# Two quads of weights multiplied in plain fp32, and the loads of w_ada spread among them

## The chip, the cores and the metric

One core of one Trainium2 chip runs the kernel. The metric is the device time of one execution in microseconds (us); less is better. A core has TensorE (PE, with its weight loads as PEld), VectorE (DVE), ScalarE (ACT), GpSimd (POOL) and SyncE (SP), which here issues the transfers.

## What the reference computes

One decoder layer on 256 tokens of width 2048, in fp32:

```python
mod = jax.nn.silu(c) @ w_ada + b_ada                # w_ada 2048 x 6144
shift, scale, gate = jnp.split(mod, 3, axis=-1)
h = _rms_norm(x, g_norm) * (1.0 + scale[:, None, :]) + shift[:, None, :]
proj = h @ w_in                                     # w_in 2048 x 9296
...                                                 # 8 + 8 heads: DSA top-k and MoBA attention, SiLU gates
y = jnp.concatenate([ya, yb], axis=-1) @ w_out      # w_out 2048 x 2048
return x + gate[:, None, :] * y
```

`h` can't be multiplied before the columns of `w_ada` that make its shift and scale have been loaded and summed.

## The kernel before

**Units.** The 2048 inputs of `w_in` are 16 k-tiles of 128 rows. Its columns are 19 groups: z, q, k, v of four quads (b0, b1, a0, a1), 512 columns each, and three index groups i0, i1, i2 of 384, 384 and 336. The unit of the schedule is one k-tile by 512 columns; the projection has 290.5 of them.

**Split products.** An fp32 number is kept as two parts in fp32r: `hi`, a copy rounded by ACT, and `lo`, the rest, made by DVE. A product of weights and `h` is the three matmuls hi*hi, hi*lo, lo*hi (L760, L761, L762) for each of the two tiles of 128 tokens (t). Weights are split by `cast_hi` (L306, ACT, into `wh`) and `cast_lo` (L316, DVE, into `wl`), two cast units ahead of the matmuls (`LA`); `h` is split in `build_h` (L391, L392, L397 for k-tile 0; L394, L395, L397 after).

**Modulation.** A load of w_ada holds 128 of its columns over all rows (1 MB); `gemv` (L273, DVE) sums it with s = silu(c). Chunk 0 is k-tile 0, chunk 1 k-tile 1, then two k-tiles each, with a shift and a scale load for each k-tile. Once a chunk's last sum is there, its k-tiles of h are built.

**Passes.** A planner, run while the program is built, orders the loads. A column group takes, in its turn, those k-tiles whose modulation is known, and adds the result to what it had (`evac`: the first pass copies on ACT, L662; later ones add on DVE, L664). A quad whose four groups take one k-tile is one load of 1 MB, "a quad"; both first quads, b1 and a0, are of this kind with k-tile 0. When all 16 k-tiles are known, the turns go by `FINAL`, and attention runs between the matmuls of this last stretch. The output projection follows.

**Buffers and queues.** All loads of w_ada, w_in and w_out share four buffers of 1 MB (`raw`); SP issues them in their order, each when the load four before it has been used up: by `gemv`, or by the last `cast_lo`. `wh` and `wl` have four buffers each, the products' PSUM tiles (`mm`) four. In the start, `in_order` fixes the order of instructions on the engines: x is scaled by its rsqrt (L350), transposed on PE (L360, `ptx`) and copied with the gain (L365, `xnT`).

Of the kernel before, what the change touches and what calls it, by code (L numbers as in the profile page):

```python
# [49 lines left out]
def hybrid_block(ctx: ExitStack, tc: tile.TileContext, x, cols, w_ada_t, w_in, w_out, out):  # L50
# [58 lines left out]
    # s = silu(c), and the products of the head gains with -1/sqrt(HD)  # L109
# [23 lines left out]
    def rsqrt(dst, ssq, n):  # L133
        # dst = (ssq / n + eps) ** -0.5
# [9 lines left out]
    # a load of w_ada: 128 of its columns, over all rows; h0, h1 bound the part of the rows  # L144
# [38 lines left out]
    while turn:  # L183
        while ready and (ready[0][0] <= n_kt or known == pos[turn[0]]):
# [38 lines left out]
    # the first weights come before the last part of the first chunk of the modulation  # L223
# [5 lines left out]
    def issue(upto):  # L229
        nonlocal n_issued  # L230
        while n_issued < min(upto, len(loads)):
            ld = loads[n_issued]
            raw = rawp.tile([P, 2048], F32, tag="raw", name=f"raw{n_issued}")
# [6 lines left out]
            elif ld["kind"] == "quad":  # L240
                # the column groups of a quad are 1024 apart
# [5 lines left out]
                if n_issued == n_start - 1:  # L247
                    # its first group, and the others behind the next load
# [42 lines left out]
    def cast_hi(j):  # L291
# [62 lines left out]
    def x_transpose(k2):  # L354
        # the transpose of two k-tiles of x, each token scaled by its rsqrt
# [13 lines left out]
    def start_mod():  # L369
        # what is known of the first chunk's modulation before its last part  # L370
# [108 lines left out]
    def prep(q, c):  # L479
        # sums of squares of the heads, their rsqrt, and the scaled heads (in place)  # L480
# [160 lines left out]
    with in_order():  # L641
        for j in range(1, LA):
# [161 lines left out]
```

## Time and profile before

| what | us |
|---|---|
| median of 3 runs | 579.33 |
| their range | 578.39 to 579.95 |
| span of the profiled execution | 577.5 |
| PE busy | 550.7 |
| DVE busy | 443.4 |
| ACT busy | 325.4 |

No time of its own is given for the profiled execution: its span, 577.5, runs from its first to its last record, and the median of the runs, 579.33, stands 1.8 above it. Busy times overlap, so they don't add to the span.

### The profile page before, as it was taken

How to read it: one execution, taken by the hardware profiler on the slowest of the kernel's cores; microseconds unless marked ns; L12 is line 12 of the kernel's file. 1: busy time of each engine (PE TensorE's matmuls, PEld its weight loads, DVE VectorE, ACT ScalarE, POOL GpSimd, SP SyncE). 2: the span in 40 equal slices, each digit the busy share in tenths (PEclk: the TensorE clock that was granted, in tenths of full speed). 3: DMA queues.
4: the chain of work that ended last, by engine and by line, in shares of the span. 5: the costliest groups of instructions: out<-in, count | busy, mean ns of one | idle time of the engine just before them, and what ended most of it. 6: DMA issues, size and time to landing. Idle time of an engine off the chain costs nothing.

```text
span 577.5 us, 7394 instructions
## 1 busy us (share of the span) xinstructions
PE 550.7 (95%) x2626; PEld 457.4 (79%) x2626; DVE 443.4 (77%) x675; ACT 325.4 (56%) x667; POOL 49.3 (9%) x61
## 2 busy tenths in 40 slices
PE   2869999999999999998999999999999999999996
PEld 2548888888878998976768888888877888887885
DVE  4876879898899797888979995788668576458452
ACT  5898563434435353567655567555766785554340
POOL 4100000000000000102101012010330210000000
PEclk8789999999999999999999999999999999999999
DMA  8988988989998898887864476777556468445701
GB/s 290 370 298 316 396 330 305 337 322 345 351 346 273 338 344 315 306 312 268 297 236 159 150 276 239 247 281 273 212 182 219 146 228 282 145 150 190 245 36 36
DMA packets 59669, 150.08 MB, mean 260 GB/s; under 512 B 3056, under 2 KB 9456, under 8 KB 53616
## 3 DMA queue, kind: packets, MB, share of 16 engines
q1 hardware_dynamic: 58480, 147.51, 71.4%
q10 hardware_dynamic: 1152, 2.10, 1.2%
q8 instruction: 20, 0.33, 0.2%
q14 instruction: 17, 0.14, 0.1%
HBM read 147.50 MB, written 2.10 MB: 259 GB/s over the span
## 4 chain that ended last, share of the span: by engine, by line
PE 80%; ACT 8%; DVE 4%; DMA 3%; POOL 2%; issue 2%; SPq 0%; DVEq 0%; ACTq 0%; POOLq 0%
PE mm_y_o L760 5%; PE mm_y_o L761 5%; PE mm_y_o L762 5%; PE mm_h_qa L760 2%; PE mm_h_ka L761 2%; PE mm_h_qa L762 2%; PE mm_h_qa L761 2%; PE mm_h_ka L762 2%; PE mm_h_ka L760 2%; PE mm_h_za L761 2%; PE mm_h_i L760 2%; PE mm_h_zb L762 2%; PE mm_h_zb L761 2%; PE mm_h_qb L760 2%; PE mm_h_qb L761 2%; PE mm_h_qb L762 2%
## 5 line engine op out<-in xcount | busy, mean ns | idle before, releaser
L306 ACT ACTIVATE wh<-raw 128x1024 fp32r<-128x1024 f32 (+3 forms) x192 | 187.1, 993 | 158.2 <-DMA raw<-in_w_in 60.6
L316 DVE TENSOR_TENSOR wl<-raw,wh 128x1024 fp32r<-128x1024 f32 (+3 forms) x192 | 215.2, 1140 | 61.9 <-ACT wh L306 61.4
L273 DVE CUSTOM_DVE_ANT_0 raw<-raw,s_row 128x2048 f32<-128x2048 f32 (+1 forms) x49 | 110.6, 2257 | 13.9 <-DMA raw<-in_w_ada_t 13.8
L760 PE MATMUL mm_y_o<-wh,yT 128*128 128x512 f32 x128 | 51.7, 404 | 0.0
L761 PE MATMUL mm_y_o<-wl,yT 128*128 128x512 f32 x128 | 49.9, 390 | 0.0
L762 PE MATMUL mm_y_o<-wh,yT 128*128 128x512 f32 x128 | 49.8, 390 | 0.0
L760 PE MATMUL mm_h_i<-wh,hhi 128*128 128x384 f32 (+1 forms) x96 | 31.5, 333 | 0.5 <-DVE p_i L664 0.5
L762 PE MATMUL mm_h_i<-wh,hlo 128*128 128x384 f32 (+1 forms) x96 | 31.5, 329 | 0.0
L761 PE MATMUL mm_h_i<-wl,hhi 128*128 128x384 f32 (+1 forms) x96 | 31.5, 328 | 0.0
L760 PE MATMUL mm_h_za<-wh,hhi 128*128 128x512 f32 x64 | 26.3, 413 | 4.6 <-ACT wh L306 4.6
L762 PEld LDWEIGHTS mm_y_o<-wh,yT 128*128 128x128 f32 x128 | 24.0, 188 | 5.3 <-DVE yT L554 0.2
L760 PEld LDWEIGHTS mm_y_o<-wh,yT 128*128 128x128 f32 x128 | 24.1, 188 | 4.8 <-ACT yT L553 0.2
L761 PEld LDWEIGHTS mm_y_o<-wl,yT 128*128 128x128 f32 x128 | 24.1, 188 | 4.6
L760 PE MATMUL mm_h_kb<-wh,hhi 128*128 128x512 f32 x64 | 26.0, 406 | 0.2 <-ACT p_zb L662 0.2
L760 PE MATMUL mm_h_vb<-wh,hhi 128*128 128x512 f32 x64 | 25.7, 403 | 0.2 <-ACT p_qb L662 0.2
L760 PE MATMUL mm_h_zb<-wh,hhi 128*128 128x512 f32 x64 | 25.9, 408 | 0.0
L761 PE MATMUL mm_h_za<-wl,hhi 128*128 128x512 f32 x64 | 25.7, 402 | 0.1
L760 PE MATMUL mm_h_qb<-wh,hhi 128*128 128x512 f32 x64 | 25.7, 401 | 0.0
L760 PE MATMUL mm_h_qa<-wh,hhi 128*128 128x512 f32 x64 | 25.7, 409 | 0.0
L760 PE MATMUL mm_h_ka<-wh,hhi 128*128 128x512 f32 x64 | 25.4, 402 | 0.0
L762 PE MATMUL mm_h_za<-wh,hlo 128*128 128x512 f32 x64 | 25.3, 398 | 0.0
L760 PE MATMUL mm_h_va<-wh,hhi 128*128 128x512 f32 x64 | 25.2, 397 | 0.0
(215 smaller groups left out, 1208.4 us busy)
## 6 DMA issues: line engine op xcount, KB each, us to landing
raw<-in_w_in SPq DMA_DIRECT2D x51, 1024.0 KB, 6.0
raw<-in_w_ada_t SPq DMA_DIRECT2D x47, 1024.0 KB, 6.7
raw<-in_w_out SPq DMA_DIRECT2D x16, 1024.0 KB, 5.1
raw<-in_w_in SPq DMA_DIRECT2D x17, 512.0 KB, 4.5
raw<-in_w_in SPq DMA_DIRECT2D x11, 768.0 KB, 6.2
x<-in_x SPq DMA_DIRECT2D x8, 256.0 KB, 6.9
xr<-in_x ACTq DMA_DIRECT2D x8, 256.0 KB, 6.5
raw<-in_w_in SPq DMA_DIRECT2D x3, 672.0 KB, 5.5
```

What stands on the lines that cost most here:

```text
L273: nc.vector.tensor_tensor_reduce(out=ld["v"], in0=ld["v"], in1=s_row[:, h0:h1], scale=1.0, scalar=0.0, op0=ALU.mult, op1=ALU.add, accum_ou ...
L306: nc.scalar.activation(hi[:, :n, :w], v, AF.Copy)
L316: nc.vector.tensor_tensor(lo[:, :n, :w], v, sb["hi"][:, :n, :w].bitcast(F32), op=ALU.subtract)
L760: nc.tensor.matmul(ps, a_hi, sb["hi"][:, i, :w], start=st, stop=False)
L761: nc.tensor.matmul(ps, a_hi, sb["lo"][:, i, :w], start=False, stop=False)
L762: nc.tensor.matmul(ps, a_lo, sb["hi"][:, i, :w], start=False, stop=en)
```

## The change

Both first quads are loaded into buffers of the pool that holds the weights' parts (one tile now holds `hi` and `lo` together, four buffers as before), not into `raw`, and their products are single matmuls of plain fp32 (`whole`): no cast, and `h` of k-tile 0 not split until the fifth cast unit (`SPLIT_AT`), when `split_h(0)` makes the parts for the later passes. The loads of w_ada come at places of their own (`ADA_FIRST`), where four stood together; chunk 1 counts as known once its loads are placed, and loads of w_ada are pulled forward where the next group could otherwise take no new k-tile. Removed comments are left out here.

```diff
-ADA_AT, ADA_FIRST, ADA_GAP, ADA_LAG, GATE_AT, GATE_GAP = 4, 4, 5.5, 2, 150, 8
+ADA_FIRST, ADA_GAP, ADA_LAG, GATE_AT, GATE_GAP = (4, 8, 8, 11, 14.5, 18), 5.5, 2, 150, 8
...
+    def w_tile(name):
+        return wsp.tile([P, 2, 2, 512], F32R, tag="w", name=name)
...
+    ada_at = list(ADA_FIRST)
+    ada_at += [ADA_FIRST[-1] + ADA_GAP * (i + 1) for i in range(len(ada) - len(ada_at))]
...
-        if ada and n_kt >= ada_at:
-            for _ in range(ADA_FIRST if ada_at == ADA_AT else 1):
-                ld = ada.pop(0)
-                loads.append(ld)
-                if "end" in ld:
-                    ready.append((n_kt + ADA_LAG, CHUNKS[ld["end"]][1]))
-            ada_at += ADA_GAP
+        if ada and n_kt >= ada_at[0]:
+            ada_at.pop(0)
+            ld = ada.pop(0)
+            loads.append(ld)
+            if "end" in ld:
+                ready.append((n_kt + (ADA_LAG if ld["end"] > 1 else 0), CHUNKS[ld["end"]][1]))
...
     while turn:
+        while ada and (n_kt >= ada_at[0] or (known == pos[turn[0]] and not ready)):
+            ada_at[0] = min(n_kt, ada_at[0])
+            between()
...
-            raw = rawp.tile([P, 2048], F32, tag="raw", name=f"raw{n_issued}")
+            if ld["kind"] == "quad":
+                raw = w_tile(f"quad{n_issued}").rearrange("p c k n -> p (c k n)").bitcast(F32)
+            else:
+                raw = rawp.tile([P, 2048], F32, tag="raw", name=f"raw{n_issued}")
...
+        if sb["whole"]:
+            return
...
-        hi = wsp.tile([P, 2, 512], F32R, tag="wh", name=f"wh{j}")
-        nc.scalar.activation(hi[:, :n, :w], v, AF.Copy)
-        sb["hi"] = hi
+        sb["hi"], sb["lo"] = w_tile(f"w{j}").rearrange("p c k n -> c p k n")
+        nc.scalar.activation(sb["hi"][:, :n, :w], v, AF.Copy)
...
-            hhi[k] = h_tile(f"hhi{k}", F32R)
             if b == 0:
-                nc.scalar.activation(hhi[k], xnT[k], AF.Identity, bias=sh, scale=am)
                 nc.vector.tensor_scalar(xnT[k], xnT[k], am, sh, op0=ALU.mult, op1=ALU.add)
...
+    SPLIT_AT = 4
...
+        if j == SPLIT_AT:
+            with in_order():
+                split_h(0)
...
+            if sb["whole"]:
+                nc.tensor.matmul(ps, xnT[k][:, ts_], ld["v"][:, i, :w], start=st, stop=en)
+                continue
             nc.tensor.matmul(ps, a_hi, sb["hi"][:, i, :w], start=st, stop=False)
```

Line numbers move: L391/L392 become L409, L397 becomes L392, L306 L320, L316 L330, L662 L675, L664 L677, L273 L284, and the plain products stand in L782.

**The first quad on PE.** Names are tiles: `mm_h_zb` is the product of group z of quad b1, `ptx` the transposes of x. Before, from the fifth matmul of the first quad on:

```order
L761 MATMUL mm_h_zb_0_265<-wl_218,hhi_242 128x512
L760 MATMUL mm_h_zb_1_266<-wh_216,hhi_242 128x512
L762 MATMUL mm_h_zb_0_265<-wh_216,hlo_245 128x512
L761 MATMUL mm_h_zb_1_266<-wl_218,hhi_242 128x512
L762 MATMUL mm_h_zb_1_266<-wh_216,hlo_245 128x512
L760 MATMUL mm_h_qb_0_292<-wh_247,hhi_242 128x512
L761 MATMUL mm_h_qb_0_292<-wl_249,hhi_242 128x512
L762 MATMUL mm_h_qb_0_292<-wh_247,hlo_245 128x512
L360 MATMUL ptx_277<-ident,x_2_154 128x128 x2
L760 MATMUL mm_h_qb_1_293<-wh_247,hhi_242 128x512
L761 MATMUL mm_h_qb_1_293<-wl_249,hhi_242 128x512
L360 MATMUL ptx_277<-ident,x_2_162 128x128 x2
```

In the changed kernel, from just before the quad's first product:

```order
L373 MATMUL ptx_227<-ident,x_1_152 128x128 x2
L782 MATMUL mm_h_zb_0_249<-quad_173,xnT_216 128x512
L373 MATMUL ptx_227<-ident,x_1_160 128x128 x2
L373 MATMUL ptx_232<-ident,x_1_152 128x128 x2
L373 MATMUL ptx_232<-ident,x_1_160 128x128 x2
L782 MATMUL mm_h_zb_1_250<-quad_173,xnT_216 128x512
L373 MATMUL ptx_257<-ident,x_2_154 128x128 x2
L373 MATMUL ptx_257<-ident,x_2_162 128x128 x2
L782 MATMUL mm_h_qb_0_268<-quad_173,xnT_216 128x512
L782 MATMUL mm_h_qb_1_269<-quad_173,xnT_216 128x512
```

Three matmuls for a group and tile of tokens have become one, of `xnT` itself, and the first stands among the transposes that used to come ahead of it.

**From the second quad to the first two-k-tile pass, on ACT.** Before, behind the last gains (`raw_317` is the second quad, `raw_319` the first weights of the next pass):

```order
L365 ACTIVATE xnT_389<-ptx_380,cc 128x256
L306 ACTIVATE wh_331<-raw_317 128x512
L306 ACTIVATE wh_364<-raw_317 128x512
L306 ACTIVATE wh_391<-raw_317 128x512
L306 ACTIVATE wh_407<-raw_317 128x512
L662 ACTIVATE p_za_0_403<-mm_h_za_0_395 128x512
L662 ACTIVATE p_za_1_405<-mm_h_za_1_396 128x512
L306 ACTIVATE wh_425<-raw_319 128x1024
L662 ACTIVATE p_qa_0_419<-mm_h_qa_0_411 128x512
```

In the changed kernel (`raw_289` is that next pass's first load):

```order
L378 ACTIVATE xnT_329<-ptx_320,cc 128x256
L390 ACTIVATE hhi_331<-xnT_216 128x256
L675 ACTIVATE p_za_0_339<-mm_h_za_0_335 128x512
L675 ACTIVATE p_za_1_341<-mm_h_za_1_336 128x512
L411 ACTIVATE xnT_239<-xnT_239,mmod_291 128x256
L675 ACTIVATE p_qa_0_347<-mm_h_qa_0_343 128x512
L390 ACTIVATE hhi_373<-xnT_239 128x256
L675 ACTIVATE p_qa_1_349<-mm_h_qa_1_344 128x512
L320 ACTIVATE w_360<-raw_289 128x1024
L675 ACTIVATE p_ka_0_367<-mm_h_ka_0_363 128x512
L675 ACTIVATE p_ka_1_369<-mm_h_ka_1_364 128x512
```

The casts of the quads are gone; the split of h (`hhi_331`) now stands here, and the first cast, `w_360`, stands behind the copies of the second quad's z and q (four of its eight) and ahead of those of k.

**The loads behind the quads, on SP and DVE.** Before, SP's loads from the first two-k-tile one on (`in_w_ada_t` is w_ada):

```order
L260 DMA raw_319<-in_w_in 128x2x512
L237 DMA raw_321<-in_w_ada_t 128x2048
L260 DMA raw_323<-in_w_in 128x2x512
L260 DMA raw_423<-in_w_in 128x2x512
L260 DMA raw_441<-in_w_in 128x2x512
L237 DMA raw_443<-in_w_ada_t 128x2048
L260 DMA raw_462<-in_w_in 128x2x336
L260 DMA raw_486<-in_w_in 128x2x384
L260 DMA raw_510<-in_w_in 128x4x384
L237 DMA raw_512<-in_w_ada_t 128x2048
```

In the changed kernel, from the second two-k-tile one on; `raw_353` is the scale of k-tile 2, `raw_390` and `raw_439` shift and scale of k-tile 3:

```order
L271 DMA raw_351<-in_w_in 128x2x512
L248 DMA raw_353<-in_w_ada_t 128x2048
L271 DMA raw_355<-in_w_in 128x2x512
L271 DMA raw_377<-in_w_in 128x2x512
L248 DMA raw_390<-in_w_ada_t 128x2048
L271 DMA raw_392<-in_w_in 128x2x336
L271 DMA raw_416<-in_w_in 128x2x384
L248 DMA raw_439<-in_w_ada_t 128x2048
L271 DMA raw_441<-in_w_in 128x2x384
L271 DMA raw_465<-in_w_in 128x2x512
```

And DVE there, from the split of h of k-tile 1 on (an ISA row with a `raw` is a product of w_ada, the row behind it reads its sum):

```order
L392 TENSOR_TENSOR hlo_375<-xnT_239,hhi_373 128x256
L330 TENSOR_TENSOR w_360<-raw_289,w_360 128x1024
L330 TENSOR_TENSOR w_379<-raw_351,w_379 128x1024
L284 ISA raw_353,mmod_358<-raw_353,s_row 128x2048
L284 ISA mmod_358 128x1
L330 TENSOR_TENSOR w_395<-raw_355,w_395 128x1024
L330 TENSOR_TENSOR w_418<-raw_377,w_418 128x1024
L284 ISA raw_390,mmod_358<-raw_390,s_row 128x2048
L284 ISA mmod_358 128x1
L330 TENSOR_TENSOR w_444<-raw_392,w_444 128x2x336
L330 TENSOR_TENSOR w_467<-raw_416,w_467 128x2x384
L284 ISA raw_439,mmod_358<-raw_439,s_row 128x2048
```

The shift of k-tile 3 is loaded three loads of weights later than before and its scale two, and the rest, `lo`, of i2's weights (`w_444`) stands on DVE behind the product of `raw_390`, as that of i1's, the next row, behind that of `raw_439`.

The planner's passes become 58, from 55; k-tiles 2 and 3 are used from unit 22.3 on (18.8 before), and all 16 k-tiles are known at unit 157.6 (149.9).

## Rows read from the trace of the kernel before

Times are microseconds from the start of the span unless marked ns; what stands in brackets at the end of a timeline row is the idle time of that engine before it and what ended it.

**Rows 1.** Windows of the span; x are instructions, then granted PE clock, DMA share, GB/s

```profile
0.00:35.00 35.00, 17.08 (x73) 12.62 (x73) 22.64 (x37) 25.64 (x59) 8.91 (x29) 0.85 0.93 339
...
42.00:100.00 58.00, 58.00 (x268) 49.12 (x267) 46.56 (x49) 36.77 (x56) 0.00 (x0) 1.00 0.91 335
100.00:200.00 100.00, 99.40 (x469) 84.69 (x468) 87.32 (x100) 42.90 (x54) 0.00 (x0) 1.00 0.91 330
200.00:300.00 100.00, 97.62 (x495) 80.42 (x493) 86.16 (x118) 58.30 (x126) 7.42 (x6) 1.00 0.82 297
```

**Rows 2.** Timeline of PE: the second quad, and the two-k-tile pass after it

```profile
34.54 0.64 PE L760 MATMUL mm_h_za<-wh,hhi 128*128 128x512 f32 x1 [4.59 <-ACT wh L306]
...
36.29 0.63 PE L760 MATMUL mm_h_za<-wh,hhi 128*128 128x512 f32 x1
36.71 0.63 PE L761 MATMUL mm_h_za<-wl,hhi 128*128 128x512 f32 x1
...
41.97 0.84 PE L760 MATMUL mm_h_za<-wh,hhi 128*128 128x512 f32 x2
42.64 0.40 PE L761 MATMUL mm_h_za<-wl,hhi 128*128 128x512 f32 x1
...
61.27 0.39 PE L760 MATMUL mm_h_zb<-wh,hhi 128*128 128x512 f32 x1
```

**Rows 3.** Timeline, 17 to 26 us: how the first product is reached

```profile
17.63 0.47 ACT L365 ACTIVATE xnT<-ptx,cc 128x256 f32<-128x256 f32 x1 [2.06 <-PE ptx L360]
...
18.00 1.32 ACT L350 ACTIVATE x<-x,rx 128x512 f32<-128x512 f32 x2
18.05 0.22 DVE L382 SCALAR_TENSOR_TENSOR mmod<-mmod,cc 128x1 f32<-128x1 f32 x1
...
19.85 0.41 DVE L392 TENSOR_SCALAR xnT<-xnT,mmod 128x256 f32<-128x256 f32 x1 [1.57 <-ACT hhi L391]
...
20.57 0.72 PE L760 MATMUL mm_h_zb<-wh,hhi 128*128 128x512 f32 x1
...
24.28 1.07 ACT L662 ACTIVATE p_zb<-mm_h_zb 128x512 f32<-128x512 f32 x2
...
25.24 1.22 ACT L365 ACTIVATE xnT<-ptx,cc 128x256 f32<-128x256 f32 x3
```

**Rows 4.** Timeline of PE: plain fp32 products of the heads among split ones

```profile
436.57 0.60 PE L520 MATMUL sa<-qka 128*128 128x256 f32 x2
436.81 0.58 PE L760 MATMUL mm_h_za<-wh,hhi 128*128 128x512 f32 x1
437.24 0.40 PE L761 MATMUL mm_h_za<-wl,hhi 128*128 128x512 f32 x1
437.47 0.39 PE L762 MATMUL mm_h_za<-wh,hlo 128*128 128x512 f32 x1
...
521.79 0.67 PE L542 MATMUL pva<-pTa,p_va 128*128 128x256 f32 x2
522.29 0.39 PE L544 MATMUL pva<-pTa,p_va 128*128 128x128 f32 x2
```

**Rows 5.** Transfers issued up to 50 us, median us to landing

```profile
raw<-in_w_ada_t SPq DMA_DIRECT2D x7, 1024.0 KB, 7.2
...
raw<-in_w_in SPq DMA_DIRECT2D x4, 512.0 KB, 4.6
```

**Rows 6.** Timeline: one load of w_ada issued, and its product

```profile
40.73 0.34 SPq L237 DMA_DIRECT2D raw<-in_w_ada_t  x1
...
48.48 2.29 DVE L273 CUSTOM_DVE_ANT_0 raw<-raw,s_row 128x2048 f32<-128x2048 f32 x1 [1.62 <-DMA raw<-in_w_ada_t]
```

**Rows 7.** Groups by form on DVE and ACT: busy us, mean ns

```profile
L316 DVE TENSOR_TENSOR wl<-raw,wh 128x1024 fp32r<-128x1024 f32 x152 | 183.3, 1222 | 55.4 <-ACT wh L306 55.2
...
L664 DVE TENSOR_TENSOR p_za<-mm_h_za,p_za 128x512 f32<-128x512 f32 x8 | 5.5, 686 | 1.9 <-PE mm_h_za L762 1.9
...
L306 ACT ACTIVATE wh<-raw 128x1024 fp32r<-128x1024 f32 x152 | 158.0, 1056 | 128.7 <-DMA raw<-in_w_in 46.2 <-PE mm_y_o L762 32.9 <-issue 14.2
```

More of the change, by code (lines that the diff above doesn't have):

```diff
@@ L165, in hybrid_block @@
     pos = {g: 0 for g in ORDER}
-    n_kt, ada_at, gate_at = 0, ADA_AT, GATE_AT
+    n_kt, gate_at = 0, GATE_AT
+    ada_at = list(ADA_FIRST)
+    ada_at += [ADA_FIRST[-1] + ADA_GAP * (i + 1) for i in range(len(ada) - len(ada_at))]
     def between():
-        nonlocal ada_at, gate_at
-        if ada and n_kt >= ada_at:
-            for _ in range(ADA_FIRST if ada_at == ADA_AT else 1):
-                ld = ada.pop(0)
-                loads.append(ld)
-                if "end" in ld:
-                    ready.append((n_kt + ADA_LAG, CHUNKS[ld["end"]][1]))
-            ada_at += ADA_GAP
+        nonlocal gate_at
+        if ada and n_kt >= ada_at[0]:
[4 more added lines that the diff above has]
+                ready.append((n_kt + (ADA_LAG if ld["end"] > 1 else 0), CHUNKS[ld["end"]][1]))
         elif gates and n_kt >= gate_at:
@@ L193, in hybrid_block @@
         if g[0] == "z" and end == seg0 + 1 and [pos[o] for o in gs] == 4 * [seg0]:
-            between()
             turn = [o for o in turn if o not in gs]
@@ L286, in hybrid_block @@
             for o, e in parts:
-                subs.append(dict(li=li, ld=m, o=o, e=e, first=m["first"] and o == 0, last=m["last"] and e == n))
+                subs.append(dict(li=li, ld=m, o=o, e=e, first=m["first"] and o == 0, last=m["last"] and e == n,
+                                 whole=ld["kind"] == "quad"))
     next_load = 0
@@ L312, in cast_lo @@
         sb = subs[j]
+        if sb["whole"]:
+            return
         v = sb["ld"]["v"][:, sb["o"]:sb["e"], :]
         n, w = v.shape[1], v.shape[2]
-        lo = wsp.tile([P, 2, 512], F32R, tag="wl", name=f"wl{j}")
-        nc.vector.tensor_tensor(lo[:, :n, :w], v, sb["hi"][:, :n, :w].bitcast(F32), op=ALU.subtract)
-        sb["lo"] = lo
+        nc.vector.tensor_tensor(sb["lo"][:, :n, :w], v, sb["hi"][:, :n, :w].bitcast(F32), op=ALU.subtract)
     gemv_todo = []
@@ L373, in start_mod, with split_h @@
         nc.vector.tensor_tensor(ss[:, :m], ss[:, :m], bmod[:, :m], op=ALU.add)
+    def split_h(k):
+        hhi[k] = h_tile(f"hhi{k}", F32R)
+        nc.scalar.activation(hhi[k], xnT[k], AF.Copy)
+        hlo[k] = h_tile(f"hlo{k}", F32R)
+        nc.vector.tensor_tensor(hlo[k], xnT[k], hhi[k].bitcast(F32), op=ALU.subtract)
     def build_h(b):
@@ L394, in build_h @@
                 nc.scalar.activation(xnT[k], xnT[k], AF.Identity, bias=sh, scale=am)
-                nc.scalar.activation(hhi[k], xnT[k], AF.Copy)
-            hlo[k] = h_tile(f"hlo{k}", F32R)
-            nc.vector.tensor_tensor(hlo[k], xnT[k], hhi[k].bitcast(F32), op=ALU.subtract)
+                split_h(k)
         yield 0
@@ L626, in hybrid_block @@
     with in_order():
-        cast_hi(0)
-        cast_lo(0)
         x_gain(0)
@@ L641, in hybrid_block @@
     with in_order():
-        for j in range(1, LA):
+        for j in range(LA):
             cast_hi(j)
@@ L707, in group_done @@
             bg_q.add(prep_z(g[1:]), "prepz" + g[1:])
+    SPLIT_AT = 4
+    assert all(sb["whole"] for sb in subs[:SPLIT_AT + 1])
     total = len(subs)
@@ L753, in hybrid_block @@
             ts_ = slice(t * P, (t + 1) * P)
-            if ld["kset"] == "h":
+            if sb["whole"]:
+                pass
+            elif ld["kset"] == "h":
                 a_hi, a_lo = hhi[k][:, ts_], hlo[k][:, ts_]
@@ L759, in hybrid_block @@
             en = sb["last"] and i == len(ks) - 1
+            if sb["whole"]:
+                nc.tensor.matmul(ps, xnT[k][:, ts_], ld["v"][:, i, :w], start=st, stop=en)
+                continue
             nc.tensor.matmul(ps, a_hi, sb["hi"][:, i, :w], start=st, stop=False)
```

## The prediction, made before the run

> **What bounds the kernel now.** I read the windows first, for where PE is idle. Up to 35 us it is busy for 17.1 us of 35; from 42 to 100 us for all of 58.0, and from 100 to 300 us for 197.0 of 200 [rows 1]. So from 42 us on PE is the bound, and what the change does there is worth what it adds to or takes from PE's own queue. A head start that PE has at some unit of the schedule is kept to the end, unless waits eat it; 0.3% of 579.33, 1.74 us, is about what a measurement can tell.
>
> Then I read PE's timeline around the second quad. Its first matmul, at 34.54, had waited 4.59 us for ACT's cast; the matmuls behind it start 0.42 us apart [rows 2], where the split ones at 437 us start 0.23 apart [rows 4]: for a few us PE ran at its lower level. The first two-k-tile pass, unit 8 of the schedule, begins at 41.97; after a short wait for `lo` it runs from 42.64, and unit 21.8 (zb0) begins at 61.27 [rows 2]. That is 19.3 us for 13.8 units, 1.40 a unit, with no other wait. Two things are to be found: when the changed kernel reaches unit 8, and what it waits for up to unit 22.3, where it is back in loads of four k-tiles.
>
> **The first product.** Before, it starts at 20.57, behind ACT's rounded copy of h, the cast and DVE's `lo`. The modulation is complete at 18.05 + 0.22 = 18.27, and scaling `xnT` on DVE takes 0.41 [rows 3]. Plain fp32 needs nothing else, so the first product can start at about 18.7, 1.8 us earlier.
>
> **What PE pays.** A plain product of 128x512 takes the place of three split matmuls, 3 x 0.23 = 0.69. The nearest row is the heads' plain product of 128x256: it starts at 436.57, and the split matmul behind it, 0.23 long, ends where L761 starts, at 437.24; so it took 437.24 - 0.23 - 436.57 = 0.44 [rows 4], 0.88 for 512 columns. The other pair of 256 columns, 521.79 to 522.29, gives 0.50, or 1.00 [rows 4], which is the upper bound; the lower is the 0.69 of the split. I take 0.88, since it was among other matmuls, as here. Sixteen such products add 16 x 0.19 = 3.0 us (0 to 5.0). They are no term of the sum, as ACT sets the pace (next).
>
> The Trainium skill (FP8 and Floating Point Precision, TensorE Precision Notes) says that a true fp32 product is four passes through the array, and this speaks against the change, since the split needs only three. With the pitch of 0.23 it makes an estimate of 0.92 a product and 3.7 us in all; the trace's 0.88 is near that, and the sum would be the same by either, while ACT is later.
>
> **What ACT still has to do.** Between 17.63 and the first cast of the two-k-tile pass (`w_360`) ACT's queue has: one gain (0.47), six more scalings of x at 0.66, 15 gains at 0.41, twelve copies out of PSUM at 0.54 (quad b1's eight, a0's z and q), and three activations of 128x256 to modulate and split h, priced as gains, 0.41 each [rows 3]. That is 0.47 + 3.96 + 6.15 + 6.48 + 1.23 = 18.3 us. Eight casts of the quads are gone from ACT, and with them DVE's eight `lo`. If ACT never waits, the cast starts at 35.9 and takes 1.06 [rows 7], to 37.0; one more copy frees the PSUM tile at 37.5, and `lo`, 1.22 [rows 7], ends at 38.2. Before, `lo` was there at 42.64. **The head start at unit 8 is 42.64 - 38.2 = 4.4 us**, and what PE pays for plain fp32 is in it, hidden behind ACT: fifteen products of 0.88 and a first one at the lower level, 1.76, from 18.7 on, end at 33.7 without the transposes between them, so PE has some 2 us of cover for these. Without that cover each further us of PE's would cost one.
>
> **What the loads take back.** SP's and DVE's queues now have the loads of k-tile 3's modulation closer ahead of their use. `raw_390` (its shift) can be issued when the first two-k-tile group after za1's has been split. Its cast stands behind both copies of k, 37.0 + 2 x 0.54 = 38.1, so it ends at 39.2 and `lo` at 40.4. From issue to landing a load of w_ada takes 7.2 us in the median [rows 5]; the one issued at 40.73 before was multiplied at 48.48 after DVE had waited for it, 7.75 later [rows 6]. So landing at 47.6; its product takes 2.29 [rows 6], to 49.9, and behind it on DVE is `lo` of i2's weights, 1.22 x 672/1024 = 0.8 as an estimate, to 50.7. PE gets to i2 (unit 16) at 37.5 + 8 x 1.40 = 48.7: a wait of 2.0. i1's load can't be issued before the product at 49.9, lands 4.6 later [rows 5], at 54.5, and cast and `lo` (0.8 and 0.9, from the same rows by columns) end at 56.2; PE is there at 50.7 + 2.8 x 1.40 = 54.6: a wait of 1.6. Together 3.6 us. Nothing else is queued behind these two that PE needs sooner.
>
> The other bound: the load of w_ada lands as fast as one of 512 KB, in 4.6 [rows 5]. Then the shift lands at 45.0, its product ends at 47.3, `lo` of i2 at 48.1, in time for 48.7; i1's load is issued at 47.3 and ready at 53.6, where PE wants it at 52.6: 1.0. The waits are 1.0 to 3.6, and I take the middle, 2.3: the bytes in flight are about those of before, but the load of the shift has fewer others behind it.
>
> The Trainium skill (DMA: Bandwidth & Descriptors, Anatomy of one DMA — SWDGE (gpsimd) path) gives 2.0 us and the bytes over 436 GB/s for a transfer, for those that POOL issues. SP issues these; for 1 MB it makes an estimate of 4.4 us where the row has 7.2. By the page the lower bound holds and the time is 575.9; by the row it is 578.5. The row is of this queue and this stretch, so it weighs more.
>
> **What comes later.** From unit 22.3 on the loads are again those of four k-tiles and one of w_ada every 5.5 units, as before, which PE took without a wait between 42 and 100 us [rows 1]. The three more passes bring six more DVE adds of 0.69 [rows 7], 4.1 us of DVE work, spread over a stretch where DVE is busy for 80 to 87% [rows 1]; PE covers them by its two cast units ahead, and I cost them at nothing. If each were on the path, it would be 4.1. The 3.0 us that PE is idle between 100 and 300 us [rows 1] are waits for ACT and DVE at the change to the last stretch; they will move, in either direction, and I count nothing for them but allow 1 us in the range.
>
> **Sum.** 4.4 - 2.3 = 2.1 us less, so a span of 575.4 from 577.5 and, with the same 1.8 around it, 577.2 for the runs.
>
> **Rivals.** (1) The loads eat nearly all: waits of 3.6 and the late shift of k-tile 3 once more at qb0, 579.3 - 4.4 + 3.6 = 578.5 and up to 579.5, the same within what can be told. For it speaks the 7.75 us of rows 6, against it that DMA was busy for 0.91 of the stretch from 42 to 100 us [rows 1] and will have less in flight here. (2) The loads take nothing: 579.3 - 4.4 = 574.9. For it speaks that DVE has eight casts less in the start; against it that `raw_390` stands behind four loads. (3) Slower: PE's clock rises late. It was granted 0.85 on the mean up to 35 us [rows 1], and at the lower level every plain product costs 0.88 more. About 2 us of PE time are covered by ACT, so the forecast holds until the second or third such product; from the seventh or so on the change is a loss of over 0.3%, and with all eight of the first quad and half of the second it would be 577.2 + 11 x 0.88 - 2 = 584.9. For it speaks that PE starts its products earlier, with less work behind it; against it that the row of 20.57 was 0.72 long and those at 42 us 0.40 [rows 2, 3], so that the clock came up soon after the stream began, and that the wait of 4.59 which came before the second drop is gone. (4) The six adds are all on the path: 577.2 + 4.1 = 581.3.
>
> **Chances and range.** Forecast 0.43, rival 1 0.27, rival 2 0.14, rival 3 0.10, rival 4 0.06. The forecast's own range, from the middle of the waits to either side, is 576.0 to 578.3. Faster by over 0.3% is below 577.6: three quarters of the forecast (0.33) and rival 2 (0.14), 0.47. Within 0.3%: 0.10 of the forecast, 0.24 of rival 1, and 0.02 of the others: 0.36. Slower: 0.08 and 0.05 of rivals 3 and 4, 0.04 of rival 1: 0.17. The range that leaves out 2 in 10 goes from 573.9 (rival 2 with 1 us of the later waits gained) to 580.5 (rival 1 with 1 us lost).
>
> **What would show it.** The first plain product near 18.7; products 0.88 apart; no wait of PE of over 1.5 us before 36; the first split matmul of za's second pass at about 37.5 and its L785 near 38.2; a wait of PE ahead of i2 and i1 between 48 and 57, put down to DVE's `lo` behind a product of w_ada. The prediction is wrong if PE is at unit 8 later than 40 us, if the granted clock stays low past 24 us, or if PE's idle time after 60 us grows by over 2 us.

## The result, and the profile after

| kernel | median us | range, runs | ratio to before | span of the profiled execution |
|---|---|---|---|---|
| before | 579.18 | 578.39 to 579.95, 4 | 1 | 577.5 |
| changed | 585.03 | 584.31 to 585.46, 4 | 1.0099 [1.0076, 1.0121] | 583.7 |

The change makes the kernel slower by 1.0%, where 577.2 us was forecast. What stands in brackets behind a ratio is its 95% interval.

On the first page of the changed kernel's profile, the row of busy times, and the row of the chain that ended last:

```profile
PE 554.3 (95%) x2610; PEld 453.1 (78%) x2610; DVE 442.3 (76%) x673; ACT 320.5 (55%) x659; POOL 47.9 (8%) x61
...
PE 65%; DVE 14%; ACT 10%; DMA 4%; issue 3%; POOL 2%; SPq 0%; DVEq 0%; POOLq 0%; ACTq 0%
```

and that last row of the kernel before:

```profile
PE 80%; ACT 8%; DVE 4%; DMA 3%; POOL 2%; issue 2%; SPq 0%; DVEq 0%; ACTq 0%; POOLq 0%
```

So 15% of the span has left PE's part of the chain, most of it for DVE (10 points more) and ACT (2), although both are busy for no longer than before. That tells where the chain runs, not what it costs. The windows say where PE is idle; the stretches of [rows 1] in the changed kernel, and one more:

```profile
0.00:35.00 35.00, 22.34 (x76) 13.69 (x77) 17.54 (x30) 25.03 (x57) 8.73 (x29) 1.00 0.87 331
42.00:100.00 58.00, 54.17 (x243) 43.91 (x242) 47.48 (x52) 32.79 (x50) 0.00 (x0) 1.00 0.93 331
100.00:200.00 100.00, 98.99 (x471) 84.71 (x470) 86.37 (x101) 43.45 (x54) 0.00 (x0) 1.00 0.92 331
200.00:300.00 100.00, 97.54 (x478) 80.15 (x477) 85.84 (x113) 52.77 (x111) 5.27 (x6) 1.00 0.82 295
300.00:400.00 100.00, 95.57 (x479) 77.47 (x478) 87.44 (x191) 62.46 (x154) 15.02 (x12) 1.00 0.62 217
```

Up to 35 us PE is busy for 5.3 us more than before. From 42 to 100 us it is idle for 3.8 us, where before it was idle for none, and from 300 to 400 for 4.4. Before, that last stretch reads:

```profile
300.00:400.00 100.00, 99.55 (x488) 82.71 (x489) 85.90 (x181) 59.69 (x139) 13.71 (x11) 1.00 0.66 234
```

**The start was a little better than forecast.** PE's timeline, the places of [rows 2, 3]:

```profile
19.02 1.91 PE L782 MATMUL mm_h_zb<-quad,xnT 128*128 128x512 f32 x2
20.73 1.49 PE L373 MATMUL ptx<-ident,x 128*128 128x128 f32 x6
...
31.72 1.88 PE L782 MATMUL mm_h_qa<-quad,xnT 128*128 128x512 f32 x4
33.44 1.88 PE L782 MATMUL mm_h_ka<-quad,xnT 128*128 128x512 f32 x4
...
36.47 0.80 PE L784 MATMUL mm_h_za<-w,hhi 128*128 128x512 f32 x1
37.10 0.39 PE L785 MATMUL mm_h_za<-w,hhi 128*128 128x512 f32 x1
```

The first plain product stands at 19.02 (before: 20.57, split). A group's two products leave four records and take 1.72 us, 0.86 each. The wait of 4.59 us ahead of the second quad is gone, and L785 of the first two-k-tile pass starts at 37.10, 5.5 us earlier than before.

**The lead over the whole run.** From PE's timeline I counted the matmuls of `w_in` (six of 512 columns make a unit, or four plain records) and noted when each unit of the schedule begins. The lead is before's time less this kernel's. The records add up to 290.5 units in each kernel. A lead is that of one profiled execution. Columns are the unit, before's time, and leads of four kernels; the last three are experiments below:

```
unit  before  changed  plain_only  plan_only  plain_zb1_first
  18    56.0      5.3         4.4        1.5              3.9
  24    64.5      2.6         4.4        1.5              3.9
  36    80.8     -0.1         4.4       -1.3              3.9
 150   237.9     -1.5         2.6       -2.7              4.3
 186   300.9      1.3         4.0       -3.9              7.8
 234   379.1     -9.4         4.0      -13.8             -2.3
 290   473.9     -7.3         5.2      -11.9             -4.2
```

The 6.2 us of the spans come together as 2.6 ahead at unit 24, 2.8 lost up to unit 36, 1.4 up to 150, 5.8 up to 290, and 1.1 won back behind the projection: 2.62 - 2.76 - 1.36 - 5.83 + 1.14 = -6.19. (At unit 186 a lead says little, since the heads' matmuls stand elsewhere in each program.)

**Units 18 to 24: a wait of the length that was forecast.** SP's load of k-tile 3's scale, the products of its shift (44.24) and of its scale on DVE, ACT's cast of i1's weights, and PE:

```profile
44.09 0.34 SPq L248 DMA_DIRECT2D raw<-in_w_ada_t  x1
44.24 2.29 DVE L284 CUSTOM_DVE_ANT_0 raw<-raw,s_row 128x2048 f32<-128x2048 f32 x1 [0.18 <-DMA raw<-in_w_ada_t]
...
51.54 2.29 DVE L284 CUSTOM_DVE_ANT_0 raw<-raw,s_row 128x2048 f32<-128x2048 f32 x1 [2.57 <-DMA raw<-in_w_ada_t]
52.48 0.84 ACT L320 ACTIVATE w<-raw 128x768 fp32r<-128x768 f32 x1 [1.07 <-DMA raw<-in_w_in]
53.38 0.61 PE L784 MATMUL mm_h_i<-w,hhi 128*128 128x384 f32 x2 [1.45 <-ACT w L320]
53.76 0.95 DVE L330 TENSOR_TENSOR w<-raw,w 128x768 fp32r<-128x768 f32 x1
...
54.77 0.44 PE L785 MATMUL mm_h_i<-w,hhi 128*128 128x384 f32 x1 [0.78 <-DVE w L330]
```

DVE waits for the load of the scale until 51.54, 7.45 us after its issue, and `lo` of i1 stands behind the product: that is PE's second wait, 0.78. The first, 1.45, is for ACT's cast, which itself waits for i1's own weights: their load was issued at 46.57 and took 5.8 us to landing.

**Units 24 to 36: a late load, and casts behind copies.** The issue of the load of kb0's weights, then ACT, with PE and DVE:

```profile
54.74 0.37 SPq L271 DMA_DIRECT2D raw<-in_w_in  x1
...
63.65 0.60 ACT L675 ACTIVATE p_qb<-mm_h_qb 128x512 f32<-128x512 f32 x1 [3.48 <-PE mm_h_qb L786]
64.15 2.00 ACT L320 ACTIVATE w<-raw 128x1024 fp32r<-128x1024 f32 x2
65.23 2.36 DVE L330 TENSOR_TENSOR w<-raw,w 128x1024 fp32r<-128x1024 f32 x2 [2.19 <-ACT w L320]
65.25 0.74 PE L784 MATMUL mm_h_kb<-w,hhi 128*128 128x512 f32 x2 [0.28 <-ACT w L320]
66.04 0.59 ACT L675 ACTIVATE p_qb<-mm_h_qb 128x512 f32<-128x512 f32 x1
66.51 0.50 PE L785 MATMUL mm_h_kb<-w,hhi 128*128 128x512 f32 x1 [0.52 <-DVE w L330]
...
70.47 0.60 ACT L675 ACTIVATE p_kb<-mm_h_kb 128x512 f32<-128x512 f32 x1 [3.84 <-PE mm_h_kb L786]
```

and that load among the transfers, us to landing:

```profile
raw<-in_w_in SPq DMA_DIRECT2D x1, 1024.0 KB, 8.8
```

ACT is idle for 3.48 us before it copies qb0 out of PSUM, with both casts of kb0's weights queued behind that copy. But these weights landed only at 63.6, 8.8 us after the issue at 54.74, just before the copy began, so the copy holds the cast for 0.5 us, from 63.6 to 64.15, and up to 63.6 it is the load. At 70.47, for vb0, it is the queue: its weights had landed at 68.8 (issued at 60.67, 8.1 us), 1.7 us before the copy that their cast stands behind. In the program of before these casts stand ahead of the copies. From unit 24 to 36 PE is idle for 1.6 us, and its matmuls behind these waits take 1.2 us longer than before.

**The last stretch.** Who PE waits for between 255 and 370 us (us in total, times, longest), in the changed kernel:

```profile
PE mm_h_i L784 <- DVE p_i L677: 2.0, 2, 1.4
PE ptb L548 <- ACT nsb L542: 1.6, 2, 1.5
PE ptq L460 <- ACT qkb L528: 1.3, 1, 1.3
PE lg L468 <- ACT qi L462: 1.2, 1, 1.2
PE sb L534 <- ACT rl L471: 0.3, 1, 0.3
```

and before:

```profile
PE lg L453 <- ACT qi L447: 1.4, 1, 1.4
PE ptq L445 <- ACT qkb L513: 1.1, 1, 1.1
PE sb L519 <- ACT rl L456: 0.3, 1, 0.3
```

6.4 us against 2.8. The first row, 2.0 us, are adds of the index groups' results; the others are index work and b0's heads (`qi`, `rl`, `qkb`, `nsb`). From unit 150 to unit 290 PE takes 5.8 us more than before: it is idle for 7.2 us where it was 3.7, the matmuls of `w_in` take 1.4 us more, and nine more of the other matmuls lie in it, 1.0 us. One of the waits, followed back in the changed kernel:

```profile
308.72 3.49 DVE L330 TENSOR_TENSOR w<-raw,w 128x1024 fp32r<-128x1024 f32 x3
...
309.28 0.44 PE L525 MATMUL trb<-ident,p_qb 128*128 128x128 f32 x2
...
312.13 1.40 DVE L473 SCALAR_TENSOR_TENSOR sc<-rl,w,sc 128x128 f32<-128x128 f32 x4
...
313.45 0.42 DVE L527 COPY qkb<-trb 128x256 f32<-128x256 f32 x1
313.90 0.47 ACT L528 ACTIVATE qkb<-trb,gnegb 128x256 f32<-128x256 f32 x1 [3.65 <-DVE qkb L527]
...
314.43 0.44 PE L460 MATMUL ptq<-ident,p_i 128*128 128x128 f32 x2 [1.26 <-ACT qkb L528]
```

PE has transposed a head's q at 309.28, DVE comes to copy it at 313.45, behind three rests and the index scores, ACT waits 3.65 us for DVE, and PE's next transpose, one of the index work, waits for ACT's step, with projection matmuls queued behind it.

### The profile page after: what moved, and what is told of

Its sections match the earlier page's. It is cut to its first block, busy times and chain, and to the rows that moved or that the text cites. A ratio compares the mean times of both kernels' runs of the same rounds, so it can differ in the third digit from the quotient of the medians.

```text
span 583.7 us, 7346 instructions
## 1 busy us (share of the span) xinstructions
PE 554.3 (95%) x2610; PEld 453.1 (78%) x2610; DVE 442.3 (76%) x673; ACT 320.5 (55%) x659; POOL 47.9 (8%) x61
## 4 chain that ended last, share of the span: by engine, by line
PE 65%; DVE 14%; ACT 10%; DMA 4%; issue 3%; POOL 2%; SPq 0%; DVEq 0%; POOLq 0%; ACTq 0%
DVE w L330 7%; PE mm_y_o L784 5%; PE mm_y_o L785 5%; PE mm_y_o L786 5%; DMA raw<-in_w_ada_t 3%; ACT w L320 3%; DVE raw L284 2%; PE mm_h_ka L784 2%; PE mm_h_ka L785 2%; PE mm_h_ka L786 2%; PE mm_h_i L784 2%; PE mm_h_i L785 2%; PE mm_h_i L786 2%; PE mm_h_qa L785 2%; PE mm_h_qa L786 2%
## 5 line engine op out<-in xcount | busy, mean ns | idle before, releaser
L320 ACT ACTIVATE w<-raw 128x1024 fp32r<-128x1024 f32 (+3 forms) x184 | 182.5, 1006 | 149.6 <-DMA raw<-in_w_in 60.3
L330 DVE TENSOR_TENSOR w<-raw,w 128x1024 fp32r<-128x1024 f32 (+3 forms) x184 | 209.8, 1162 | 62.0 <-ACT w L320 61.5
L284 DVE CUSTOM_DVE_ANT_0 raw<-raw,s_row 128x2048 f32<-128x2048 f32 (+1 forms) x49 | 110.5, 2255 | 20.2 <-DMA raw<-in_w_ada_t 20.0
L784 PE MATMUL mm_y_o<-w,yT 128*128 128x512 f32 x128 | 51.5, 402 | 0.0
L785 PE MATMUL mm_y_o<-w,yT 128*128 128x512 f32 x128 | 49.9, 390 | 0.0
L786 PE MATMUL mm_y_o<-w,yT 128*128 128x512 f32 x128 | 49.8, 390 | 0.0
L784 PE MATMUL mm_h_i<-w,hhi 128*128 128x384 f32 (+1 forms) x96 | 31.6, 336 | 3.8 <-DVE p_i L677 2.0
L785 PE MATMUL mm_h_i<-w,hhi 128*128 128x384 f32 (+1 forms) x96 | 31.6, 330 | 0.8 <-DVE w L330 0.8
L786 PE MATMUL mm_h_i<-w,hlo 128*128 128x384 f32 (+1 forms) x96 | 31.4, 329 | 0.0
L786 PEld LDWEIGHTS mm_y_o<-w,yT 128*128 128x128 f32 x128 | 24.0, 188 | 5.3 <-DVE yT L569 0.2
L784 PEld LDWEIGHTS mm_y_o<-w,yT 128*128 128x128 f32 x128 | 24.1, 188 | 4.9 <-ACT yT L568 0.2
L785 PEld LDWEIGHTS mm_y_o<-w,yT 128*128 128x128 f32 x128 | 24.1, 188 | 4.6
L784 PE MATMUL mm_h_za<-w,hhi 128*128 128x512 f32 x62 | 25.6, 415 | 0.0
L784 PE MATMUL mm_h_qa<-w,hhi 128*128 128x512 f32 x62 | 25.2, 410 | 0.0
L785 PE MATMUL mm_h_kb<-w,hhi 128*128 128x512 f32 x62 | 24.5, 396 | 0.6 <-DVE w L330 0.5
L784 PE MATMUL mm_h_kb<-w,hhi 128*128 128x512 f32 x62 | 24.8, 407 | 0.3 <-ACT w L320 0.3
L785 PE MATMUL mm_h_za<-w,hhi 128*128 128x512 f32 x62 | 24.3, 392 | 0.6 <-DVE w L330 0.6
L784 PE MATMUL mm_h_vb<-w,hhi 128*128 128x512 f32 x62 | 24.6, 403 | 0.3 <-ACT w L320 0.3
L785 PE MATMUL mm_h_vb<-w,hhi 128*128 128x512 f32 x62 | 24.3, 392 | 0.5 <-DVE w L330 0.5
L785 PE MATMUL mm_h_zb<-w,hhi 128*128 128x512 f32 x62 | 24.3, 391 | 0.3 <-DVE w L330 0.3
```

Of the source, the lines that this page charges most:

```text
L284: nc.vector.tensor_tensor_reduce(out=ld["v"], in0=ld["v"], in1=s_row[:, h0:h1], scale=1.0, scalar=0.0, op0=ALU.mult, op1=ALU.add, accum_ou ...
L320: nc.scalar.activation(sb["hi"][:, :n, :w], v, AF.Copy)
L330: nc.vector.tensor_tensor(sb["lo"][:, :n, :w], v, sb["hi"][:, :n, :w].bitcast(F32), op=ALU.subtract)
L784: nc.tensor.matmul(ps, a_hi, sb["hi"][:, i, :w], start=st, stop=False)
L785: nc.tensor.matmul(ps, a_hi, sb["lo"][:, i, :w], start=False, stop=False)
L786: nc.tensor.matmul(ps, a_lo, sb["hi"][:, i, :w], start=False, stop=en)
```

## Experiments

Waits named below are PE's between 255 and 370 us, summed from that view as above.

**Two halves.** `plain_only` is the changed kernel with the loads and passes of before; `plan_only` is before with those of the change. The first is shown, against the changed kernel; the second has the same lines the other way round, against before:

```diff
-ADA_FIRST, ADA_GAP, ADA_LAG, GATE_AT, GATE_GAP = (4, 8, 8, 11, 14.5, 18), 5.5, 2, 150, 8
+ADA_AT, ADA_FIRST, ADA_GAP, ADA_LAG, GATE_AT, GATE_GAP = 4, 4, 5.5, 2, 150, 8
...
+        if ada and n_kt >= ada_at:
+            for _ in range(ADA_FIRST if ada_at == ADA_AT else 1):
...
-        while ada and (n_kt >= ada_at[0] or (known == pos[turn[0]] and not ready)):
```

Plain only: 

> The order of loads and passes of the kernel before, with the two first quads in plain fp32 in the parts' buffers as in the changed kernel. Theory P (the plan costs the time: late modulation of k-tile 3, casts of kb0 and vb0 behind copies on ACT, and a last stretch that begins at unit 157.6): the head start of plain fp32 stays, 574 to 577 us. Theory B (plain products and the parts' shared buffers cost it): 583 to 586, as in the changed kernel.

Plan only: 

> The order of loads and passes of the changed kernel, with the first two quads split and loaded as before. Theory P: slower than before, 584 to 588, with PE's loss after unit 190. Theory B: no slower than before, 578 to 580.

Measured: plain only 574.34 us (8 runs), ratio 0.9924 [0.9902, 0.9945]; plan only 590.14, 1.0201 [1.017, 1.0233]. Before was at 579.07 beside them. So plain products win 4.7 us and the new order of loads and passes costs 11.1 (its 590.14 lies above the 584 to 588 expected); 579.18 - 4.7 + 11.1 = 585.6, near the measured 585.03. The lead of plain only stands at 4.4 from unit 18 to 36 and at 5.2 at unit 290; its windows answer to [rows 1]:

```profile
42.00:100.00 58.00, 58.00 (x269) 48.93 (x268) 48.44 (x53) 34.35 (x52) 0.00 (x0) 1.00 0.93 343
...
300.00:400.00 100.00, 100.00 (x489) 83.59 (x488) 85.87 (x184) 59.72 (x138) 13.78 (x11) 1.00 0.65 232
```

and its waits are 1.7 us:

```profile
PE ptq L457 <- ACT qkb L525: 0.9, 1, 0.9
PE lg L465 <- ACT qi L459: 0.5, 1, 0.5
PE sb L531 <- ACT rl L468: 0.3, 1, 0.3
```

**Spread loads with the passes of before.** Both have the planner of the change, with places that give 55 passes, the same from za1 on as before. The first is shown; `shift3_later` has (4, 8, 8, 10, 12, 15, 20.5):

```diff
-ADA_FIRST, ADA_GAP, ADA_LAG, GATE_AT, GATE_GAP = (4, 8, 8, 11, 14.5, 18), 5.5, 2, 150, 8
+ADA_FIRST, ADA_GAP, ADA_LAG, GATE_AT, GATE_GAP = (4, 8, 8, 8, 10, 15, 20.5), 5.5, 2, 150, 8
```

First: 

> The changed kernel with ADA_FIRST (4, 8, 8, 8, 10, 15, 20.5): the second quad still comes ahead of three of the four first loads of w_ada, but k-tiles 2 and 3 are known at unit 18.8 again, and from za1's first load on loads and passes are those of the kernel before (55 passes). If the passes that follow from the later modulation cost the time, not that the loads stand apart: PE keeps its lead of about 5 us, 572 to 575 us. If standing apart costs it: 579 or more.

Second: 

> As spread_55_passes, with the scale of k-tile 2 and the shift of k-tile 3 one load of weights later each, the passes unchanged. If a late load of w_ada holds PE at i1 by DVE's queue: 1 to 2 us more than spread_55_passes, 574 to 577, with a wait of PE for DVE ahead of i2 or i1. If not: as spread_55_passes.

Measured: 579.48 (ten runs, 576.64 to 582.55 but for one of 586.90; 578.86 without it) and 579.83 (576.92 to 583.09), ratios 1.0006 [0.9979, 1.0032] and 1.0013 [0.999, 1.0036]: the same as before. The gain of the plain products is lost at units 6 to 24 (lead 6.4 at 6 and 0.1 at 24 in the first, of which the fastest execution was profiled, 5.0 and -2.3 in the second): PE waits 1.6 us for ACT's cast of za1's weights in the first, and of ka1's in the second. Both times vary more than those of the other kernels. But from unit 150 to 290 neither loses anything (0.9 to 2.6, and -2.6 to -0.7), and their waits are 1.8 and 1.7 us. So loads that stand apart don't by themselves cause the loss in the last stretch.

**The casts of kb0 and vb0 ahead of the copies.** ACT's casts and copies of cast units 15 to 21 keep the order in which they are written:

```diff
+            with pinned(PIN0 <= j < PIN1):
+                cast_hi(j + LA)
...
+            with pinned(PIN0 <= j < PIN1):
+                evac(ld)
```

> The changed kernel with ACT's queue held in the program's order over six cast units (zb0 to vb0): the casts of kb0 and vb0 ahead of the copies of qb0 and kb0. If the copies ahead of the casts cause PE's waits between 62 and 78 us: about 2.5 us less, 582 to 583, and PE at unit 36 with a lead of 1 to 3 us over before. If the loads land late anyway: as the changed kernel, 585.

Measured: 583.82 us (581.16 to 585.25), 1.0079 [1.0053, 1.0105], 1.2 us less than the changed kernel, with ranges that overlap, and 0.8 above the 582 to 583 expected. The windows from 62 to 80 us, of the changed kernel and of this one:

```profile
62.00:80.00 18.00, 16.40 (x69) 12.32 (x68) 13.13 (x13) 9.48 (x13) 0.00 (x0) 1.00 0.90 334
```

```profile
62.00:80.00 18.00, 18.00 (x81) 14.93 (x80) 14.89 (x14) 9.71 (x13) 0.00 (x0) 1.00 0.99 359
```

The waits are gone and 12 matmuls more are done, 12 x 0.23 = 2.8 us. Of this the profiled execution, the slowest of the five, keeps half: its lead at unit 36 is 1.2, where the changed kernel's is -0.1, since it lost 1.4 us more between units 18 and 24 (last section). What the other executions lost there no profile shows. Nor is the whole gain the queue's: with that loss PE comes to kb0 1.3 us later than in the changed kernel, which gives the late load that much more time. ACT's cast of kb0's weights still waits for it:

```profile
63.38 2.01 ACT L335 ACTIVATE w<-raw 128x1024 fp32r<-128x1024 f32 x2 [1.79 <-DMA raw<-in_w_in]
```

**The last stretch, moved.** `gap_5_3` begins it at unit 149.6, as before, `gap_4_8` has w_ada loads closer and 55 passes, `index_after_kb1` starts the index work when kb1 is done:

```diff
-ADA_FIRST, ADA_GAP, ADA_LAG, GATE_AT, GATE_GAP = (4, 8, 8, 11, 14.5, 18), 5.5, 2, 150, 8
+ADA_FIRST, ADA_GAP, ADA_LAG, GATE_AT, GATE_GAP = (4, 8, 8, 11, 14.5, 18), 5.3, 2, 150, 8
```

(4.8 in place of 5.3 in `gap_4_8`), and

```diff
-        if g == "i2":
+        if g == "kb1":
```

> The changed kernel with one number changed, the distance of the loads of w_ada 5.3 units for 5.5: the same passes up to unit 111, then all 16 k-tiles known at unit 149.6 in place of 157.6, 57 passes. If the late begin of the last stretch costs the 7 us that PE loses after unit 190: 577 to 580. If it is not that (theory B, or the passes as such): 583 to 586.

> The changed kernel with the loads of w_ada 4.8 units apart for 5.5: 55 passes, all k-tiles known at unit 145.9, then i1 done at 154.5, kb0 at 170.5, kb1 at 216.5, nearly the distances of the kernel before (158.5, 174.5, 218.5) in place of 170.5, 182.5, 210.5. If the attention's work crowded between i1 and kb1 costs PE the 6 us after unit 186: PE's lead falls by less than 2 us from unit 150 to the end, 578 to 581. If the 6 us are lost in another way: 584 or more.

> The changed kernel with the index scores and the top-k started when kb1 is done (unit 210.5) and not when i2 is done, so that they don't fall together with the preparation of b0 and b1. Crowding there costs the 6 us: 580 to 582. It does not, or the crowd is only moved: 584 to 587.

Measured: 586.60 (1.0123 [1.0104, 1.0142]), 591.91 (1.0213 [1.0174, 1.0253]) and 596.23 (1.0305 [1.0273, 1.0337]). The first loses 6.7 us from unit 150 to 290 (-2.8 to -9.4): that the stretch begins later is not the cause. The second lies 11 us above the 578 to 581 of its first theory: it loses 7.3 us between units 72 and 150, where w_ada loads are denser, and 3.6 from 150 to 290. In its last stretch the groups have nearly the units left that they had before (8.6 of index groups, then 2, 2, 12, 12, 12, 12; before 8.6, 2, 2, 12, 12, 12, 10), and its waits are 5.5 us all the same. So these distances alone don't spare a kernel the waits.

The third lies above both of its ranges. Between units 210 and 246 its lead goes from -2.0 to -21.1, but 13.8 us of that are matmuls other than those of `w_in` (162, for 56 before), the index work among them, that now stand there. From unit 150 to 290 it loses 14.5 us, and PE is idle for 11.0 us, 8.4 of them up to unit 210, before any index work runs, for b0's heads, the gate and adds. So the waits come without index work beside them too.

**The order of groups in the last stretch.** These four change only `FINAL`. In `z_between` (from the changed kernel) and `plain_z_between` (from plain only):

```diff
-FINAL = ["i2", "i0", "i1"] + [c + q for q in QUADS for c in "zqkv"]
+FINAL = ["i2", "i0", "i1", "zb0", "qb0", "kb0", "vb0", "za0", "za1"]
+FINAL += [c + q for q in QUADS for c in "zqkv" if c + q not in FINAL]
```

In `plain_zb1_first` (from plain only) the list is `["zb1", "i2", "i0", "i1"]`, in `b0_apart` (from the changed kernel) `["i2", "i0", "i1", "zb0", "qb0", "za1", "kb0", "za0", "vb0"]`, with the same line behind it.

> The changed kernel with the two z groups of quads a0 and a1 taken, in the last stretch, between v of b0 and z of b1 (18 units of matmuls with little work behind them), so that q and k of b1 end 18 units later against the index work, as far as they do before; all loads and passes up to unit 157.6 as in the changed kernel. Crowding theory (the loss after unit 186 comes from b1's work on DVE and ACT falling on the index work): PE loses under 2 us between units 186 and 290 in place of 6, so 579 to 582 us. Rival (the loss is the number of passes and DVE adds, whatever the order): 584 to 586. Rival (b1's heads are then late at the end): over 586.

> Plain quads with all loads and passes of before up to unit 149.9, but in the last stretch z of b1 (12 units) stands ahead of the index groups, so that index work and b0's groups begin 12 units later and k of b1 ends where it did: the distance from the index groups to b1's q and k is 12 units shorter, in the direction of the changed kernel. Crowding theory: 3 to 6 us of the gain of plain quads are lost, 577 to 580 us. Rival (number of passes): 574 to 575, as plain quads alone.

> Plain quads with all loads and passes of before up to unit 149.9, and the z groups of a0 and a1 between v of b0 and z of b1. Crowding theory: PE's waits of 262 to 300 us shrink, 572 to 574 us, the fastest so far; rival (b1's and a0's work, moved by 18 and 8 units, is then late at the end): 575 to 580.

> The changed kernel with, in the last stretch, z of a1 (8 units) between q and k of b0 and z of a0 (10 units) between k and v of b0, so that k of b0 ends 20 units after the index groups (12 in the changed kernel, 16 before) and v of b0 12 after k (2 in the changed kernel, 12 before); all loads and passes up to unit 157.6 as in the changed kernel. Theory that b0's preparation falls on the index work: PE's waits between 255 and 370 us go from 6.4 us back to about 2 or 3, and the time is 579 to 582 us. Rival (any order other than the one of before costs as much, since index work begins 8 units later than before): 584 to 587.

Measured, with the waits:

```
z_between        585.96 us  1.0122 [1.0091, 1.0154]  waits 5.0
plain_zb1_first  582.46 us  1.0059 [1.0041, 1.0078]  waits 7.3
plain_z_between  573.95 us  0.9913 [0.989, 0.9935]   waits 1.8
b0_apart         585.76 us  1.0122 [1.0104, 1.0141]  waits 6.5
```

`plain_zb1_first` has every load and pass of plain only up to unit 149.9, 55 passes, and one group of 12 units in another place, and loses 8.1 us against it, more than was expected. Its waits are of the kinds of the changed kernel, but for the adds of `p_i`:

```profile
PE lg L466 <- ACT qi L460: 3.1, 2, 2.1
PE ptq L458 <- ACT qkb L526: 2.8, 1, 2.8
PE ptk L449 <- ACT kk L444: 1.1, 1, 1.1
PE sb L532 <- ACT rl L469: 0.3, 1, 0.3
```

So the order of the groups alone moves the time by more than the change does, with no pass added. `FINAL` is the same before and after, though: what differs in the changed kernel is how many units each group has left when the stretch begins (12.9 of index groups, then 4, 4, 4, 2 for z, q, k, v of b0; before 8.6, then 2, 2, 12, 12). So `plain_zb1_first` shows that such a loss can come from the order, and not that this is what costs in the changed kernel. Both attempts to mend the changed kernel by distance (b1 further from the index work, b0 spread out) failed: 585.96 and 585.76, as their rivals had it. `plain_z_between` is the fastest, with plain only 0.4 us behind, which their ranges don't tell apart.

## Why the prediction was wrong

**Right in size: the first product, the price of a product, the head start.** 18.7 was forecast and 19.02 measured; 0.88 a product and 0.86. The Trainium skill (FP8 and Floating Point Precision, TensorE Precision Notes) has four passes for a true fp32 product; by the pitch of 0.23 that made an estimate of 0.92, and the trace agrees within 7%. The head start at unit 8 was 5.5 us for a forecast 4.4, as ACT's first cast came at 34.34, not 35.9, and with `plain_only` the whole of the plain products was 4.7 us in the medians.

One step of it did not hold: "ACT sets the pace". PE was busy without a wait from 22 to 37 us, and reached the first split product at 36.47, 1.0 us after its cast had ended. The "2 us of cover" were used up by the transposes between the products, 3.0 us. What PE pays for plain fp32 was on the path, then; it did no harm to the forecast, since ACT was quicker too.

**Right in size, in part by luck: what the loads take back.** 2.3 us were forecast for i2 and i1; PE waited 2.2, and the lead fell from 5.3 to 2.6, near the 2.1 of the forecast. But the load that was to hold both, the shift of k-tile 3, landed in 5.5 us, and its product ran at 44.24, not after 47.6: PE had no wait at i2. At i1 it was i1's own load (5.8 us for the 4.6 taken) and the product of the next load, k-tile 3's scale, which the sum did not have. That one took 7.45 us to be usable, by the row (7.2), not by the estimate of 4.4 that was worked out from the Trainium skill (DMA: Bandwidth & Descriptors, Anatomy of one DMA — SWDGE (gpsimd) path).

**Wrong: "What comes later".** "From unit 22.3 on the loads are again those of four k-tiles [...], which PE took without a wait", and the new passes were costed "at nothing". That the loads are of the same kind says nothing of where their casts stand in ACT's queue, nor of which groups end when. Of the loss, two parts are placed:

- Units 24 to 36, 2.8 us: kb0's load lands late, 8.8 us after its issue, and the casts of kb0 and vb0 stand behind copies that wait for PE. At vb0 that held the cast for 2.1 us after the weights were there, at kb0 for 0.5; with the casts ahead of the copies (`casts_first`) these waits are gone. The order was in the program and could have been read before the run; the forecast read ACT's queue only up to the first two-k-tile pass.
- Units 150 to 290, 5.8 us: PE is idle for 3.5 us more, and between 255 and 370 us it waits for adds, index work and b0's heads for 6.4 us where it was 2.8. That the new order of loads and passes brings this is shown from both sides, by `plain_only` and `plan_only`; `spread_55_passes` and `shift3_later`, with the passes of before from za1 on, wait 1.8 and 1.7 us there and lose nothing, so it is not the spreading as such; and `plain_zb1_first` waits 7.3 and loses 8.1, so a loss of this size needs no added pass. My sentence that these waits "will move, in either direction", with 1 us for it, named the place and mis-sized it nearly sixfold.

What stays open is what in the new order does it. The begin of the stretch (`gap_5_3`), the distance from the index work to b1 (`z_between`) and that of b0's groups from each other (`b0_apart`) were each put back and won no time; `gap_4_8` waits although its groups stand nearly as before; `index_after_kb1` waits with no index work beside it. The 2.0 us for adds of `p_i` come in each of `plan_only`, `z_between` and `b0_apart` too, and in this stretch in no kernel with the passes of before, so the added passes may have their part. The chain at 308 to 314 us, DVE late for ACT and ACT late for PE, is how it looks on the engines; why `plain_only` escapes it was only argued. The 1.4 us between units 36 and 150 (0.5 of them idle time) were not followed further.

**The rivals.** Rival 1 had a load late once more, though at kb0 and not at qb0, but its time was 578.5 to 579.5. Rival 3 fell: the first product took 1.71 us and the second 1.10, and every one from 23.54 on 0.86. That its 584.9 lies next to the measured 585.03 is chance. Rival 4, six adds on the path for 4.1, may have its place in PE's 2.0 us of waits for `p_i`'s adds, which before doesn't have there; a kernel without these passes lost more in another way, which leaves it open. Of the three signs named against the prediction the last one came: PE was idle for 9.9 us between 62 and 520 us, where it was 4.3.

## What to carry to other kernels

When a planner's table moves, cost the whole order that comes out of it and not the stretch at the table's numbers: here the plain products won 4.7 us and the new order of loads and passes cost 11.1. In queues that run in order, look for a copy that waits for PE ahead of work that PE needs next; the listing of the program shows it before any run. Split a change into its halves first: plain products with the old order beat both kernels at once.

## What was not expected of the hardware

The clock after a wait differs between executions at the same place. The changed kernel and `casts_first` wait alike at i1 (1.45 and 0.78, and 1.43 and 0.81), and then the first goes on with 0.17 us a matmul of 384 columns, the second with 0.32, at the lower level: the granted clock from 52 to 58 us was 0.74. In `casts_first`:

```profile
54.65 0.49 PE L801 MATMUL mm_h_i<-w,hhi 128*128 128x384 f32 x1 [0.81 <-DVE w L345]
54.93 0.52 PE L802 MATMUL mm_h_i<-w,hlo 128*128 128x384 f32 x1
55.25 0.52 PE L800 MATMUL mm_h_i<-w,hhi 128*128 128x384 f32 x1
```

So a wait of PE's can cost more than its length: 1.4 us more of the lead went here than in the changed kernel.

At the start the granted clock of a stretch did not tell the pace of its matmuls. Between 10 and 22 us it was 1.00 in the profiles of the changed kernel and `z_between` and 0.50 in that of `gap_5_3`, which has the same loads and passes there, yet the first plain product, begun at 19.02, 19.06 and 19.70, took 1.7 us in all three, twice the 0.86 of the later ones. The leads at unit 6 were 5.8, 6.0 and 4.9, and 0.7 of that difference is the later begin. A head start read from one profile is uncertain by that much, and the medians are the better measure.
